# A decoder block with product-key experts: twelve more U chunks ahead, sixteen more gathered rows in the gate stage, and the gathered block closed inside the dense loop

## The chip, the cores and the metric

The kernel runs on one core of a Trainium2 chip. The metric is the device time of one execution, in microseconds (us); runs of the same kernel are compared by their median. The engines are named as in the profile: PE (TensorE, matmuls; PEld its weight loads), DVE (VectorE), ACT (ScalarE), POOL (GpSimd), and SP, whose queue issues most transfers.

## What is computed

The reference is one layer of a decoder block on x (1, 512, 1024) in float32. Its second half holds most of the work around the change:

```python
def peer_ffn(h, wq, subkeys, u, v):
    q = (h @ wq).reshape(B, S, PEER_HEADS, 2, PEER_QDIM // 2)
    sub_scores = jnp.einsum('bshpk,hpnk->bshpn', q, subkeys).astype(jnp.float32)
    ...
    best_v, best_pos = lax.top_k(cand, PEER_TOPK)
    expert = jnp.take_along_axis(cand_i, best_pos, axis=-1)
    gates = jax.nn.softmax(best_v, axis=-1).astype(h.dtype)
    ...
        ub = jnp.take(u, eb, axis=0)
        hid = jax.nn.gelu(jnp.einsum('tkd,td->tk', ub, xb), approximate=False) * gb
        vb = jnp.take(v, eb, axis=0)
        return jnp.einsum('tk,tkd->td', hid, vb)
...
    h2 = rms_norm(x, norm2_w[l]) * (1.0 + scale2) + shift2
    x = x + gate2 * peer_ffn(h2, peer_wq[l], peer_subkeys[l], peer_u[l], peer_v[l])
return rms_norm(x, final_norm_w)
```

Each token picks 8 x 16 = 128 of 16384 experts; an expert is a row of U and a row of V. Ahead of it stand windowed attention, gated linear attention and their projections, which the change does not touch.

## The kernel before

The 512 tokens are four blocks of 128. Three of them (DENSE, blocks 0 to 2) are computed densely: all experts for all tokens, with a gate of zero where an expert wasn't chosen. The fourth (GB, block 3) is gathered: for each of the 128 choices s an indirect transfer on POOL's queue fetches one row of U per token (gu, L993), DVE forms the dot product with the token (L1003), ACT the gelu of eight such columns at a time (hg, L1006), a second transfer fetches the rows of V (gv, L1011), and DVE adds them, weighted, to gacc (L1016). The last 16 tokens of block 2 have their U side done by gathered rows too (the sp rows, L964).

The 16384 experts are 128 chunks of 128. For a chunk c, u_part (from L691) loads U, splits it into a high and a low half (hilo: ACT writes uc..h at L64, DVE the difference uc..l at L65), runs 24 matmuls of 128x368 into ph (L69 to L71), and takes ACT's gelu (ge, L705). v_part (from L1149) splits V the same way (vc..h, vc..l), multiplies the gates with ge (DVE L1169), and splits the product into Ah (ACT L1173) and Al (DVE L1174). v_matmuls runs 18 matmuls of 128x512 into six accumulators acc0 to acc5, two for each dense block. High and low halves share a ring of four tiles between U and V chunks; Ah and Al have four buffers each.

The work runs in stages. A front (about 290 us) with the attention; the routing heads and top-k; a gate stage (about 460 to 705 us) that builds the dense gates: gate_group (from L904) makes one-hots on DVE (o12 at L895, o2 at L911), multiplies them on PE (pg, L918), copies them on ACT (gs, L920) and stores them in DRAM (Gd). Then the dense stage (from about 736 us) goes over the chunks in order.

U chunks can be done ahead of the dense stage, since U needs no gates. AHEAD lists them: all 64 even chunks. Their gelu results go to DRAM (gsp) and come back as gel tiles. The first 11 are done beside the routing heads; the others are woven into the gate stage by a balance: every piece of work has a DVE and a PE price, and a U chunk is put in where PE's sum lags behind DVE's, by the totals DVE_ALL and PE_ALL. The first 8 gathered rows of U are fetched and multiplied in the third block of the gate stage, one for each q (a q is a group of 16 tokens). The odd U chunks are done in the dense loop, LEAD = 8 chunks ahead of their V chunk, one for every two V chunks. The remaining gathers are dealt out evenly over the chunks (gather_to), up to chunk 123.

After chunk 123 finish(GB) forms the gathered block's result: times the second gate, plus x (L1192, L1193), ACT's squares (L1194), their root by ACT's logarithm and exponential and five small DVE steps (rstd_of, L80 to L86), the scaling (L1203; for one block L1200 on ACT and L1201 on POOL), and the store. The last four chunks (LAST) run block by block, each followed by its finish.

On DVE and POOL the order in the gate stage is that of the code (manual_schedule); elsewhere a scheduler with a simulated timeline orders each engine's instructions at build time, and each engine then runs its list in that order. A wait that an instruction needs holds all that stands behind it on its engine.

Of the kernel before, what the change touches and what calls it, by code (L numbers as in the profile page):

```python
# [7 lines left out]
F32 = mybir.dt.float32  # L8
# [9 lines left out]
P = 128  # L18
# [11 lines left out]
GB = 3  # L30
TG = 16
NGRP = TD // TG
TS = 16
TU = TD - TS
NGU = TU // TG
# [3 lines left out]

AHEAD = tuple(range(0, P, 2))  # L40
RING = 6
# [5 lines left out]
def peer_block_kernel(ctx: ExitStack, tc: tile.TileContext, a: dict, out: bass.AP):  # L47
    nc = tc.nc
    cp = ctx.enter_context(tc.tile_pool(name="cp", bufs=1, side="left"))
    st = ctx.enter_context(tc.tile_pool(name="st", bufs=1, side="left"))  # L50
    dr = ctx.enter_context(tc.tile_pool(name="dr", bufs=1, space=bass.MemoryType.DRAM))
# [636 lines left out]

    gsp = dr.tile([len(AHEAD), P, TU], F32, name="gsp")
    ges, last_gelu = {}, {}  # L690

    def u_part(c, lo_eng=None, after=None):
# [12 lines left out]
        last_gelu["u"] = nc.scalar.activation(gef, ph, AF.Gelu)  # L705
        if c % 2 == 0:
            nc.scalar.dma_start(gsp[c // 2], gef)
        else:
            ges[c] = ge
# [267 lines left out]
    NS = P  # L977
# [10 lines left out]

    EARLY = 8

# [27 lines left out]

    VLAG = 10
    gathers = [(s * 0.88 / NS, gather_u, s) for s in range(NS)]  # L1020
    gathers += [((s + VLAG) / (NS + VLAG), gather_v, s) for s in range(NS)]
    gathers = [g[1:] for g in sorted(gathers, key=lambda g: g[0])]

    def gather_to(upto):
        while gather_to.n < min(upto, len(gathers)):
            f, s = gathers[gather_to.n]
            f(s)
            gather_to.n += 1
# [54 lines left out]
    def ahead(s0, n):  # L1083
        for s in range(s0, s0 + n):
            fetch_u(s)
        yield 0, 0

    def dots_of(s0, n):
        gather_to(s0 + n)
        yield 1.15 * n, 0  # L1090

    def woven(n, rows, extra):
        for q in range(P // TG):
# [4 lines left out]
            if q in extra:  # L1098
# [6 lines left out]
                    6: [gate_parts(SB)], 7: [gate_rest(SB)]}  # L1105
    third_block = {0: [ahead(0, 1)]}
    for q in range(1, EARLY):
        third_block[q] = [dots_of(q - 1, 1), ahead(q, 1)]
    third_block[EARLY - 1] += [dots_of(EARLY - 1, 1)]
    work = chain(route_heads(), *head, woven(0, rows, first_block), woven(1, rows, second_block),  # L1110
                 woven(SB, [], third_block))
    NL_U = len(AHEAD) - LAST_U
    DVE_ALL = 11 + 4 * 7.6 + 3 + 1.15 * TS + 2.82 * 2 * NGRP + 9 + 1.14 * (NL_U - WQ_U)
    PE_ALL = 1.4 * 2 * NGRP + 3 + UCOST * (NL_U - WQ_U)
# [34 lines left out]
    def v_part(c):  # L1149
# [10 lines left out]
        vh, vl = hilo(v_part.raw[:, c % 2], [P, D], f"vc{c}", nc.vector)  # L1160
        if c % 2 == 0:
            if c % 4 == 0:
                v_part.ge = dnA.tile([P, 2, TU], F32, tag="gel", bufs=2, name=f"gel{c}")
                nc.sync.dma_start(v_part.ge, gsp[c // 2:c // 2 + 2].rearrange("c p t -> p c t"))
            ge = v_part.ge[:, c // 2 % 2].rearrange("p (g t) -> p g t", g=NGU)
        else:
            ge = ges.pop(c)
# [6 lines left out]
        nc.vector.tensor_tensor(grp(Al), A, grp(Ah), OP.subtract)  # L1174
        return c, Ah, Al, vh, vl

    def v_matmuls(parts, blocks=range(len(DENSE)), qs=(0, 1)):
# [27 lines left out]

    LEAD = 8
    for c in range(1, 1 + LEAD, 2):
        u_part(c)
    for c in range(P - LAST):
        if c % 2 == 0 and c + 1 + LEAD < P:  # L1210
            u_part(c + 1 + LEAD)
        with tc.issue_after(last_gelu["u"].ins) if c < 2 else nullcontext():
            parts = v_part(c)
        v_matmuls([parts])
        gather_to(len(gathers) * (c + 1) // (P - LAST))
        if c == 16:
            tc.keep_in_program_order(bcast_load(fwb, a["fw"], D))
        if c == P - 16:
# [4 lines left out]
            for q in range(2):  # L1223
# [3 lines left out]
                nc.scalar.activation(h2n[:, q * 512:(q + 1) * 512], pb, AF.Copy)  # L1227
    with tc.issue_after(last_gelu["u"].ins), tc.issue_after(last_gelu["hg"].ins):
        nc.scalar.preload_act_table_set("natural_log_exp_and_others")
    finish(GB, [gacc[:, 0:512], gacc[:, 512:1024]])  # L1230
    last = [v_part(c) for c in range(P - LAST, P)]
# [64 lines left out]
```

## Time and profile before

| | |
|---|---|
| median of 3 runs | 1524.5 us (1523.61 to 1525.55) |
| the profiled execution | 1523.26 us |
| its span, first to last instruction | 1521.5 us, mean granted clock 0.991 |
| PE busy | 1460.3 us (96%) |
| DVE busy | 1251.6 us (82%) |
| ACT busy | 677.7 us (45%) |
| POOL busy | 482.2 us (32%) |
| bytes moved | 417.04 MB, mean 274 GB/s |

All times in the views are of the profiled execution, from its span's start. A row of the timeline has the start, the duration, the engine, the line, the operation with output and inputs, and in brackets the idle time ahead of it with what ended it. A row of the groups has the busy time, the mean of one, and the idle time ahead. A row of the waits has who waited for whom, the total, the number and the longest. Matmul ends are modelled, and some matmul records are missing from the trace.

### The profile page before, as it was taken

The page shows a single profiled execution, that of the slowest core. Times are in us where ns is not written, and L with a number is a line of the kernel's source. Part 1 is how long each engine was busy: PE and PEld are TensorE (multiplying, and loading weights), DVE is VectorE, ACT ScalarE, POOL GpSimd, SP SyncE. Part 2 cuts the span into 40 slices and gives each one's busy share as a digit, 9 for nine tenths or more (in the row PEclk, how much of TensorE's full clock was granted, in tenths as well). Part 3 has the DMA queues.
Part 4 walks back from the last instruction along what each step waited for, and adds up shares of the span by engine and source line. Part 5 has one row for each costly group of instructions (what it writes and reads, how often), then busy time and mean ns, then how long its engine had stood idle before and what let it go on. Part 6 is the DMA issues. An engine that isn't in the chain of part 4 may idle for free.

```text
span 1521.5 us, 24401 instructions
## 1 busy us (share of the span) xinstructions
PE 1460.3 (96%) x9387; PEld 1301.7 (86%) x9387; DVE 1251.6 (82%) x2389; ACT 677.7 (45%) x1072; POOL 482.2 (32%) x344
## 2 busy tenths in 40 slices
PE   4999989899999999999999999999999999999995
PEld 3787877888999999999888888888888888888884
DVE  7578657689999999996778878787878878788998
ACT  5545486533344665765333333333333333333332
POOL 1000000145505220222334434453535434454461
PEclk9999999999999999999999999999999999999997
DMA  9253535462446997899999989989999898998894
GB/s 349 99 208 115 175 106 191 152 215 92 140 171 207 305 314 229 257 295 330 411 408 335 334 317 345 357 322 333 343 349 344 326 339 344 357 335 291 312 356 157
DMA packets 158004, 417.04 MB, mean 274 GB/s; under 512 B 11312, under 2 KB 78144, under 8 KB 145472
## 3 DMA queue, kind: packets, MB, share of 16 engines
q1 hardware_dynamic: 107296, 258.18, 47.5%
q0 software_dynamic: 39312, 144.20, 25.9%
q10 hardware_dynamic: 11280, 13.11, 2.5%
q8 instruction: 73, 1.20, 0.3%
q14 instruction: 43, 0.35, 0.1%
HBM read 374.01 MB, written 41.42 MB: 273 GB/s over the span
## 4 chain that ended last, share of the span: by engine, by line
PE 89%; DVE 4%; ACT 3%; DMA 2%; issue 2%; SPq 0%; DVEq 0%; POOL 0%; ACTq 0%; POOLq 0%
PE ph L71 11%; PE ph L69 11%; PE acc L70 11%; PE acc L69 11%; PE ph L70 11%; PE acc L71 11%; PE pg L918 4%; PE pq L69 2%; PE pq L71 2%; PE pq L70 2%; PE pj L71 1%; PE pj L69 1%; PE pj L70 1%; DMA gu<-in_u_dram,ix_u 1%; PE pn L69 1%
## 5 line engine op out<-in xcount | busy, mean ns | idle before, releaser
L993 POOL DMA_INDIRECT gu<-in_u_dram,ix_u x128 | 191.4, 1495 | 314.4 <-DVE gacc L1016 128.8
L1011 POOL DMA_INDIRECT gv<-in_vP_dram,ix_v x128 | 176.8, 1381 | 216.2 <-DVE gu L1003 163.9
L1173 ACT ACTIVATE Ah<-gr 128x384 fp32r<-128x384 f32 x128 | 67.1, 525 | 308.6 <-PE acc L70 305.0
L1016 DVE SCALAR_TENSOR_TENSOR gacc<-gv,hg,gacc 128x1024 f32<-128x1024 f32 x127 | 162.8, 1282 | 0.2
L1003 DVE SCALAR_TENSOR_TENSOR gu<-gu,h2n 128x1024 f32<-128x1024 f32 x128 | 156.0, 1220 | 0.7 <-DMA gu<-in_u_dram,ix_u 0.7
L705 ACT ACTIVATE ge<-ph 128x368 f32<-128x368 f32 x128 | 59.9, 468 | 152.8 <-PE ph L71 152.7
L1174 DVE TENSOR_TENSOR Al<-gr,Ah 128x384 fp32r<-128x384 f32 x128 | 71.0, 556 | 66.4 <-ACT Ah L1173 66.2
L920 ACT ACTIVATE gs<-pg 128x512 f32<-128x512 f32 x96 | 94.1, 1114 | 3.8 <-PE pg L918 2.8
L1066 POOL IOTA iot<- 128x256 bf16 x1 | 1.5, 1540 | 282.2 <-DVE h2Tl L680 282.2
L911 DVE TENSOR_TENSOR o<-o,gp 128x3072 bf16<-128x3072 bf16 x48 | 84.0, 1755 | 0.4 <-PE pg L918 0.4
L959 POOL DMA_INDIRECT spr<-in_u_dram,spix x16 | 40.6, 2535 | 105.6 <-DVE spr L964 61.3
L918 PE MATMUL pg<-o,o 128*128 128x128 bf16 x1152 | 72.7, 218 | 0.5 <-ACT gs L920 0.5
L918 PEld LDWEIGHTS <-o 128*128 128x128 bf16 x1152 | 66.2, 97 | 6.0 <-issue 0.7
L895 DVE TENSOR_TENSOR o<-iot,t 128x2048 bf16<-128x2048 bf16 x48 | 58.4, 1223 | 2.4 <-PE pg L918 2.4
L1169 DVE TENSOR_TENSOR gr<-ge,gr 128x368 f32<-128x368 f32 x64 | 34.5, 540 | 23.3 <-ACT ge L705 23.3
L217 DVE SCALAR_TENSOR_TENSOR macc<-wa,scs,macc 128x1024 f32<-128x1024 f32 x28 | 38.8, 1385 | 5.1 <-DMA wa<-in_w_ada_dram 4.8
L1169 DVE TENSOR_TENSOR gr<-gel,gr 128x368 f32<-128x368 f32 x64 | 31.9, 535 | 2.9 <-DMA gr<-Gd 2.9
L70 PE MATMUL pq<-h2Tl,wq_0h 128*128 128x512 f32 (+1 forms) x80 | 27.9, 349 | 1.2 <-DVE h2Tl L680 1.2
L69 PE MATMUL pq<-h2Th,wq_0h 128*128 128x512 f32 (+1 forms) x80 | 28.0, 352 | 1.0 <-ACT qha L758 1.0
L71 PE MATMUL pq<-h2Th,wq_1l 128*128 128x512 f32 (+1 forms) x80 | 28.1, 352 | 0.0
L70 PE MATMUL pq<-h2Tl,wq_1h 128*128 128x512 f32 (+1 forms) x80 | 28.1, 352 | 0.0
L69 PE MATMUL pq<-h2Th,wq_1h 128*128 128x512 f32 (+1 forms) x80 | 28.0, 350 | 0.0
(2608 smaller groups left out, 5028.3 us busy)
## 6 DMA issues: line engine op xcount, KB each, us to landing
u<-in_uT_dram SPq DMA_DIRECT2D x64, 1024.0 KB, 8.3
v<-in_vP_dram SPq DMA_DIRECT2D x64, 1024.0 KB, 7.5
Gd<-gs SPq DMA_DIRECT2D x23, 1024.0 KB, 8.1
gr<-Gd SPq DMA_DIRECT2D x15, 1536.0 KB, 11.0
wa<-in_w_ada_dram SPq DMA_DIRECT2D x20, 1024.0 KB, 6.3
gsp<-ge ACTq DMA_DIRECT2D x64, 184.0 KB, 4.6
gel<-gsp SPq DMA_DIRECT2D x32, 368.0 KB, 4.8
wi<-in_w_in_dram SPq DMA_DIRECT2D x9, 1024.0 KB, 6.2
```

What stands on the lines that cost most here:

```text
L69: nc.tensor.matmul(acc, lh, rh, start=start, stop=False)
L70: nc.tensor.matmul(acc, lh, rl, start=False, stop=False)
L71: return nc.tensor.matmul(acc, ll, rh, start=False, stop=stop)
L911: nc.vector.tensor_tensor(o2, o12[:, :, 1, None].to_broadcast([P, H, 3, P, 2]), gp3[:, g0:g0 + H, :, None].to_broadcast([P, H, 3, P, 2]), ...
L918: nc.tensor.matmul(pt[:, i, :], o12[:, g, 0, :, r], o2[:, g, m, :, r], start=(m == 0), stop=(m == 2))
L920: nc.scalar.activation(gs[:, :, t0 + 4 * f:t0 + 4 * f + 4].rearrange("p b a -> p a b"), pt, AF.Copy)
L993: nc.gpsimd.indirect_dma_start(out=ur, out_offset=None, in_=a["u"], in_offset=bass.IndirectOffsetOnAxis(ap=ix_u[:, s:s + 1], axis=0))
L1003: nc.vector.scalar_tensor_tensor(ur, ur, 1.0, h2n, op0=OP.mult, op1=OP.mult, accum_out=hid[:, s:s + 1])
L1011: nc.gpsimd.indirect_dma_start(out=vr, out_offset=None, in_=a["vP"], in_offset=bass.IndirectOffsetOnAxis(ap=ix_v[:, s:s + 1], axis=0))
L1016: nc.vector.scalar_tensor_tensor(gacc, vr, hg[:, s:s + 1], gacc, op0=OP.mult, op1=OP.add)
L1173: nc.scalar.activation(grp(Ah), A, AF.Copy)
L1174: nc.vector.tensor_tensor(grp(Al), A, grp(Ah), OP.subtract)
```

## The change

Six groups of four chunks (m = 3, 8, 13, 18, 23, 28) have their two odd U chunks done ahead as well: 13, 15, 33, 35, 53, 55, 73, 75, 93, 95, 113, 115. gsp and the gel tiles are arranged for it. The gathered rows of U in the gate stage go from 8 to 24, two for each of twelve places from the second block's q = 3 on. In the dense loop the gathers are dealt out by PE's time (4.09 for a V chunk, UCOST = 4.0 more where a U chunk goes along) and end with chunk 118; finish(GB) and the load of ACT's table for logarithm and exponential go into the loop at chunk 119.

```diff
-AHEAD = tuple(range(0, P, 2))
+ODD_AHEAD = tuple(range(3, 32, 5))
+AHEAD = tuple(c for m in range(P // 4) for c in (4 * m, 4 * m + 2) + ((4 * m + 1, 4 * m + 3) if m in ODD_AHEAD else ()))
...
-    gsp = dr.tile([len(AHEAD), P, TU], F32, name="gsp")
+    gsp = dr.tile([P // 4, 2, 2, P, TU], F32, name="gsp")
...
-        if c % 2 == 0:
-            nc.scalar.dma_start(gsp[c // 2], gef)
+        if c in AHEAD:
+            nc.scalar.dma_start(gsp[c // 4, c % 2, c // 2 % 2], gef)
...
-    EARLY = 8
+    EARLY = 24
...
-    VLAG = 10
-    gathers = [(s * 0.88 / NS, gather_u, s) for s in range(NS)]
-    gathers += [((s + VLAG) / (NS + VLAG), gather_v, s) for s in range(NS)]
+    gathers = [(-1, gather_u, s) for s in range(EARLY)]
+    gathers += [((s - EARLY) * 0.88 / (NS - EARLY), gather_u, s) for s in range(EARLY, NS)]
+    gathers += [((s + 0.5) / NS, gather_v, s) for s in range(NS)]
...
-    third_block = {0: [ahead(0, 1)]}
-    for q in range(1, EARLY):
-        third_block[q] = [dots_of(q - 1, 1), ahead(q, 1)]
-    third_block[EARLY - 1] += [dots_of(EARLY - 1, 1)]
+    third_block = {}
+    places = [(second_block, q) for q in range(3, 8)] + [(third_block, q) for q in range(P // TG)]
+    for i, (block, q) in enumerate(places):
+        pieces = block.setdefault(q, [])
+        if i:
+            pieces.append(dots_of(2 * i - 2, 2))
+        if i < EARLY // 2:
+            pieces.append(ahead(2 * i, 2))
+    assert EARLY == 2 * len(places) - 2
...
-    DVE_ALL = 11 + 4 * 7.6 + 3 + 1.15 * TS + 2.82 * 2 * NGRP + 9 + 1.14 * (NL_U - WQ_U)
+    DVE_ALL = 11 + 4 * 7.6 + 3 + 1.15 * TS + 2.82 * 2 * NGRP + 1.15 * EARLY + 1.14 * (NL_U - WQ_U)
...
-            if c % 4 == 0:
-                v_part.ge = dnA.tile([P, 2, TU], F32, tag="gel", bufs=2, name=f"gel{c}")
-                nc.sync.dma_start(v_part.ge, gsp[c // 2:c // 2 + 2].rearrange("c p t -> p c t"))
-            ge = v_part.ge[:, c // 2 % 2].rearrange("p (g t) -> p g t", g=NGU)
+        if c in AHEAD:
+            if c % 4 < 2:
+                v_part.ge[c % 2] = dn.tile([P, 2, TU], F32, tag=f"gel{c % 2}", bufs=2 - c % 2, name=f"gel{c}")
+                nc.sync.dma_start(v_part.ge[c % 2], gsp[c // 4, c % 2].rearrange("c p t -> p c t"))
+            ge = v_part.ge[c % 2][:, c // 2 % 2].rearrange("p (g t) -> p g t", g=NGU)
...
-    LEAD = 8
+    LEAD, LAST_G = 8, 118
+    cost = [4.09 + (UCOST if c % 2 == 0 and c + 1 + LEAD < P and c + 1 + LEAD not in AHEAD else 0) for c in range(LAST_G)]
     for c in range(1, 1 + LEAD, 2):
         u_part(c)
     for c in range(P - LAST):
-        if c % 2 == 0 and c + 1 + LEAD < P:
+        if c % 2 == 0 and c + 1 + LEAD < P and c + 1 + LEAD not in AHEAD:
             u_part(c + 1 + LEAD)
         with tc.issue_after(last_gelu["u"].ins) if c < 2 else nullcontext():
             parts = v_part(c)
         v_matmuls([parts])
-        gather_to(len(gathers) * (c + 1) // (P - LAST))
+        gather_to(EARLY + int((len(gathers) - EARLY) * sum(cost[:c + 1]) / sum(cost) + 1e-6))
+        if c == LAST_G + 1:
+            with tc.issue_after(last_gelu["u"].ins), tc.issue_after(last_gelu["hg"].ins):
+                nc.scalar.preload_act_table_set("natural_log_exp_and_others")
+            finish(GB, [gacc[:, 0:512], gacc[:, 512:1024]])
...
-    with tc.issue_after(last_gelu["u"].ins), tc.issue_after(last_gelu["hg"].ins):
-        nc.scalar.preload_act_table_set("natural_log_exp_and_others")
-    finish(GB, [gacc[:, 0:512], gacc[:, 512:1024]])
```

Where the order moves. The line numbers of the changed kernel are higher by 1 (hilo, u_part) to 8 (finish). On ACT around V chunk 28, before (vc28h is the high half of V chunk 28, Ah that of the gates, ge37 the gelu of U chunk 37):

```order
L705 ACTIVATE ge33_9548<-ph33_9523 128x368
L64 ACTIVATE vc26h_9657<-v26_9653 128x1024
L1173 ACTIVATE Ah28_9765<-gr3_9247 128x384
L64 ACTIVATE vc27h_9690<-v26_9653 128x1024
L1173 ACTIVATE Ah29_9798<-gr3_9247 128x384
L64 ACTIVATE uc37h_9725<-u37_9723 128x1024
L705 ACTIVATE ge35_9651<-ph35_9626 128x368
L1173 ACTIVATE Ah30_9864<-gr3_9247 128x384
L64 ACTIVATE vc28h_9758<-v28_9756 128x1024
L64 ACTIVATE vc29h_9793<-v28_9756 128x1024
L1173 ACTIVATE Ah31_9900<-gr3_9247 128x384
```

And of the change:

```order
L65 ACTIVATE uc37h_10059<-u37_10057 128x1024
L1179 ACTIVATE Ah29_10135<-gr3_9651 128x384
L1179 ACTIVATE Ah30_10198<-gr3_9651 128x384
L1179 ACTIVATE Ah31_10234<-gr3_9651 128x384
L706 ACTIVATE ge37_10088<-ph37_10063 128x368
L1007 ACTIVATE hg_2440<-hid_2439 128x8
L65 ACTIVATE vc28h_10092<-v28_10090 128x1024
L65 ACTIVATE vc29h_10130<-v28_10090 128x1024
L65 ACTIVATE uc39h_10160<-u37_10057 128x1024
```

vc28h stood ahead of ge37 and Ah31, and now stands behind both and behind hg. On PE the last matmuls of U chunk 37 (into ph37) stand right ahead of V chunk 28, before:

```order
L69 MATMUL ph37_9729<-h2Th_2428,uc37h_9725 128x368
L70 MATMUL ph37_9729<-h2Tl_2429,uc37h_9725 128x368
L71 MATMUL ph37_9729<-h2Th_2428,uc37l_9726 128x368
L69 MATMUL acc0_8177<-vc28h_9758,Ah28_9765 128x512
L70 MATMUL acc0_8177<-vc28l_9759,Ah28_9765 128x512
L71 MATMUL acc0_8177<-vc28h_9758,Al28_9766 128x512
```

And of the change:

```order
L70 MATMUL ph37_10063<-h2Th_2428,uc37h_10059 128x368
L71 MATMUL ph37_10063<-h2Tl_2429,uc37h_10059 128x368
L72 MATMUL ph37_10063<-h2Th_2428,uc37l_10060 128x368
L70 MATMUL acc0_8625<-vc28h_10092,Ah28_10099 128x512
L70 MATMUL acc1_8626<-vc28h_10092,Ah28_10099 128x512
L70 MATMUL acc2_8627<-vc28h_10092,Ah28_10099 128x512
```

U chunk 37 is ahead of V chunk 28 in both; the changed kernel runs the six products with the high half first. Ahead of U chunk 37 it has V chunks 22 to 27 with no U chunk between 22 and 27; the same pattern stands at 42, 62, 82 and 102, and V chunks 3 to 6 follow each other too. On ACT around V chunk 6, before:

```order
L1173 ACTIVATE Ah6_8636<-gr0_8348 128x384
L64 ACTIVATE vc5h_8565<-v4_8528 128x1024
L1173 ACTIVATE Ah7_8669<-gr0_8348 128x384
L64 ACTIVATE uc15h_8598<-u13_8495 128x1024
L705 ACTIVATE ge13_8526<-ph13_8501 128x368
L1173 ACTIVATE Ah8_8739<-gr1_8439 128x384
L64 ACTIVATE vc6h_8631<-v6_8629 128x1024
L64 ACTIVATE vc7h_8664<-v6_8629 128x1024
```

And of the change:

```order
L706 ACTIVATE ge11_8895<-ph11_8870 128x368
L1179 ACTIVATE Ah6_9041<-gr0_8796 128x384
L1179 ACTIVATE Ah7_9071<-gr0_8796 128x384
L1179 ACTIVATE Ah8_9141<-gr1_8899 128x384
L1179 ACTIVATE Ah9_9176<-gr1_8899 128x384
L65 ACTIVATE vc6h_9036<-v6_9034 128x1024
L65 ACTIVATE vc7h_9066<-v6_9034 128x1024
```

vc6h now stands behind Ah9, which needs the buffer that V chunk 5 frees. At the end, on DVE around the gathered block's finish (y3 is its result, y0 to y2 those of the dense blocks), before:

```order
L1016 SCALAR_TENSOR_TENSOR gacc_8184<-gv125_14579,hg_2440,gacc_8184 128x1024
L1016 SCALAR_TENSOR_TENSOR gacc_8184<-gv126_14582,hg_2440,gacc_8184 128x1024
L1016 SCALAR_TENSOR_TENSOR gacc_8184<-gv127_14585,hg_2440,gacc_8184 128x1024
L1192 TENSOR_TENSOR y3_14589<-gacc_8184,h2n_2430 128x512 x2
L1192 TENSOR_TENSOR y0_14681<-acc0_8177,h2n_2430 128x512
L1192 TENSOR_TENSOR y0_14681<-acc1_8178,h2n_2430 128x512
L1192 TENSOR_TENSOR y1_14730<-acc2_8179,h2n_2430 128x512
L1192 TENSOR_TENSOR y1_14730<-acc3_8180,h2n_2430 128x512
L1193 TENSOR_TENSOR y3_14589<-y3_14589,xf3_14590 128x512 x2
```

And of the change:

```order
L1017 SCALAR_TENSOR_TENSOR gacc_8632<-gv127_14408,hg_2440,gacc_8632 128x1024
L1200 TENSOR_TENSOR y3_14499<-gacc_8632,h2n_2430 128x512 x2
L1180 TENSOR_TENSOR Al125_14657<-gr15_14237,Ah125_14656 128x384
L1201 TENSOR_TENSOR y3_14499<-y3_14499,xf3_14500 128x512
L66 TENSOR_TENSOR vc124l_14641<-v124_14638,vc124h_14640 128x1024
L1201 TENSOR_TENSOR y3_14499<-y3_14499,xf3_14500 128x512
L66 TENSOR_TENSOR vc125l_14652<-v124_14638,vc125h_14651 128x1024
L1180 TENSOR_TENSOR Al126_14668<-gr15_14237,Ah126_14667 128x384
L66 TENSOR_TENSOR vc126l_14663<-v126_14660,vc126h_14662 128x1024
L1203 TENSOR_TENSOR ssf3_14502<-ssf3_14502 128x1
```

The gathered rows (gacc) now end ahead of the low half of chunk 124, and y3's steps stand among the last chunks instead of behind them.

More of the change, by code (lines that the diff above doesn't have):

```diff
@@ L1160, in v_part @@
         vh, vl = hilo(v_part.raw[:, c % 2], [P, D], f"vc{c}", nc.vector)
-        if c % 2 == 0:
-            if c % 4 == 0:
-                v_part.ge = dnA.tile([P, 2, TU], F32, tag="gel", bufs=2, name=f"gel{c}")
-                nc.sync.dma_start(v_part.ge, gsp[c // 2:c // 2 + 2].rearrange("c p t -> p c t"))
-            ge = v_part.ge[:, c // 2 % 2].rearrange("p (g t) -> p g t", g=NGU)
+        if c in AHEAD:
[3 more added lines that the diff above has]
+            ge = v_part.ge[c % 2][:, c // 2 % 2].rearrange("p (g t) -> p g t", g=NGU)
         else:
@@ L1175, in v_part @@
         return c, Ah, Al, vh, vl
+    v_part.ge = {}
     def v_matmuls(parts, blocks=range(len(DENSE)), qs=(0, 1)):
```

## Prediction

> **What bounds the kernel now.** First the page's busy times, its chain of waits and the span:
>
> ```profile
> PE 1460.3 (96%) x9387; PEld 1301.7 (86%) x9387; DVE 1251.6 (82%) x2389; ACT 677.7 (45%) x1072; POOL 482.2 (32%) x344
> ...
> PE 89%; DVE 4%; ACT 3%; DMA 2%; issue 2%; SPq 0%; DVEq 0%; POOL 0%; ACTq 0%; POOLq 0%
> ...
> core 0: 1521.5 us, clock 0.991
> ```
>
> TensorE is 89% of the chain. Then the windows by stage (columns: us; busy and count of PE, PEld, DVE, ACT, POOL; granted clock; DMA share; GB/s) say whether it waits anywhere:
>
> ```profile
> 560.00:700.00 140.00, 139.22 (x1298) 135.61 (x1297) 131.17 (x122) 91.36 (x114) 23.56 (x10) 1.00 0.87 275
> ...
> 740.00:1440.00 700.00, 700.00 (x3432) 615.81 (x3431) 574.59 (x753) 254.10 (x360) 307.56 (x218) 1.00 0.92 342
> ```
>
> In the gate stage (upper row) PE is busy 139.22 of 140 us with DVE at 131.17; in the dense stage it is busy all of 700 us. So moving matmuls from the lower row to the upper one saves nothing by itself: PE is full in both. What can be saved is PE's idle time and what follows its last matmul. The list of PE's waits from 460 us to its end:
>
> ```profile
> PE acc L69 <- ACT Ah L1173: 1.9, 1, 1.9
> PE acc L69 <- ACT vc118h L64: 1.3, 1, 1.3
> PE ph L71 <- DVE uc124l L65: 1.0, 1, 1.0
> PE pg L918 <- ACT gs L920: 0.5, 1, 0.5
> PE tr L865 <- ACT gs L920: 0.3, 1, 0.3
> ```
>
> That is 5.0 us in all. And the end, by windows and by single instructions:
>
> ```profile
> 1503.06:1516.17 13.11, 0.00 (x0) 0.00 (x0) 12.28 (x36) 5.65 (x21) 2.93 (x2) 0.58 0.28 104
> 1516.17:1521.50 5.33, 0.00 (x0) 0.00 (x0) 0.00 (x0) 0.00 (x0) 0.00 (x0) 0.50 0.37 139
> ```
>
> ```profile
> 1502.44 0.39 PE L70 MATMUL acc<-vc127l,Ah 128*128 128x512 f32 x1
> 1502.67 0.39 PE L71 MATMUL acc<-vc127h,Al 128*128 128x512 f32 x1
> ```
>
> ```profile
> 1495.49 1.28 DVE L1016 SCALAR_TENSOR_TENSOR gacc<-gv,hg,gacc 128x1024 f32<-128x1024 f32 x1
> 1496.81 1.29 DVE L1192 TENSOR_TENSOR y<-gacc,h2n 128x512 f32<-128x512 f32 x2
> ...
> 1510.06 1.41 DVE L1203 SCALAR_TENSOR_TENSOR y<-y,rf0y,fwb 128x512 f32<-128x512 f32 x2
> ...
> 1512.74 3.43 DVE L1203 SCALAR_TENSOR_TENSOR y<-y,rf2y,fwb 128x512 f32<-128x512 f32 x2
> ```
>
> PE ends at 1502.67 + 0.39 = 1503.06; the span ends 18.44 us later, of which DVE is busy 12.28 of the first 13.11. DVE is the bound of the tail: the last gathered row is added at 1495.49, so the gathered block and the three dense blocks all finish after it.
>
> **The tail (gain).** More prices: two pieces of the chain of waits, then a short step of ACT and its scale of y1:
>
> ```profile
> 1505.65 1.33 ACT xl L1194 x4
> ...
> 1511.97 0.17 DVE rf2t L83
> ```
>
> ```profile
> 1511.50 0.20 ACT L81 ACTIVATE rf2y<-rf2m 128x1 f32<-128x1 f32 x1 [1.75 <-DVE y L1203]
> ...
> 1511.88 1.33 ACT L1200 ACTIVATE y<-y,rf1y 128x512 f32<-128x512 f32 x2
> ```
>
> In the new order the gathered block's steps stand ahead of the last chunk's low half, so they are done before PE ends. From PE's end on there is left, in the order of the new lists: the product with acc5 (half of the 1.29 of such a pair, 0.65), the scale of y0 (1.41), the last sum with x (the same shape, 0.65); then ACT's square (0.7 with its accumulator: 1.33 for two of each, above), ACT's scale of y1, which now stands ahead of the last logarithm and exponential (1.33), those two (0.2 each), six one-column steps (0.77 for four, from 1511.97 to 1512.74, and 0.3 for the others: 1.1), the scale of y2 (1.4 alone, 3.43 beside GpSimd as here).
>
> The sum is 0.65 + 1.41 + 0.65 + 0.7 + 1.33 + 0.4 + 1.1 + 1.4 = 7.6, or 9.7 with 3.43; 5.33 follows as now. That makes 13.0 to 15.0 for 18.44; I take 13.6, nearer to the lower end since GpSimd's share of y1 begins before the scale of y2 does and covers only part of it. **Gain 4.8 (3.4 to 5.4).**
>
> **The twelve U chunks (the new waits).** ACT runs its list in order. By the order of the changed kernel, between 22 and 28, 42 and 48 and so on, six V chunks follow each other with no U chunk; behind them the next chunk's high half stands behind an ACT step that needs PE to be done with all that comes before that chunk. Two places of the profile have that structure already. The first, at chunk 0, where the gelu of U chunk 9 stands ahead of vc0h (columns: start, us, engine and line, in brackets the idle time ahead and its releaser):
>
> ```profile
> 734.16 0.33 PE L71 MATMUL ph<-h2Th,uc9l 128*128 128x368 f32 x1
> 734.53 0.48 ACT L705 ACTIVATE ge<-ph 128x368 f32<-128x368 f32 x1 [3.52 <-PE ph L71]
> 734.90 1.05 ACT L64 ACTIVATE vc0h<-v 128x1024 fp32r<-128x1024 f32 x1
> ...
> 735.85 0.51 ACT L1173 ACTIVATE Ah<-gr 128x384 fp32r<-128x384 f32 x1
> 735.98 1.23 DVE L65 TENSOR_TENSOR vc0l<-v,vc0h 128x1024 fp32r<-128x1024 f32 x1 [0.40 <-ACT vc0h L64]
> ...
> 736.41 2.41 PE L69 MATMUL acc<-vc0h,Ah 128*128 128x512 f32 x6 [1.92 <-ACT Ah L1173]
> ```
>
> U's last matmul ends at 734.49; gelu and high half are done at 734.90 + 1.05 = 735.95, and with Ah PE starts at 736.41. Where Ah is done earlier, PE would start some 0.46 sooner: 1.92 − 0.46 = **1.46**. The second, at chunk 118, has Ah121 (which waits for the buffer that chunk 117 frees) ahead of vc118h:
>
> ```profile
> 1448.20 0.39 PE L71 MATMUL acc<-vc117h,Al 128*128 128x512 f32 x1
> ...
> 1449.92 1.66 PE L69 MATMUL acc<-vc118h,Ah 128*128 128x512 f32 x6 [1.33 <-ACT vc118h L64]
> ```
>
> The price there is **1.33**. One more price is that of the small gelu of the gathered rows:
>
> ```profile
> L1006 ACT ACTIVATE hg<-hid 128x8 f32<-128x8 f32 x14 | 2.9, 204 | 5.5 <-DVE gu L1003 5.2
> ```
>
> Now the new places, from the order: chunks 28, 48, 68, 88 and 108, each right behind U chunk 37, 57, 77, 97, 117 on PE, with the gelu of that chunk ahead of their high half on ACT: 5 × 1.46 = 7.3, and at 28 also the small hg gelu (0.2).
>
> Chunk 6 has Ah9 ahead of vc6h and chunk 5 ahead of it on PE: 1.33. At 118 the hg gelu comes in between (0.2), and all 18 matmuls of it now run at once. The six products with the high half take 1.4 (6 × 0.23, the spacing of the two V matmuls that end PE's work, above); the low half is due then. DVE has Al121 (0.56), a gathered row (1.28) and vc118l (1.23) to do from about 0.6 behind chunk 117's end, when Ah121 is done, so it is through at about 3.7; PE wants it at 1.53 + 1.4 = 2.9: 0.8 more. Together 1.0 over now.
>
> Sum of the new waits: 7.3 + 0.2 + 1.3 + 1.0 = **9.8** (each between 0, if the step ahead is done sooner than I read it, and 1.92, the longest such wait seen: 0 to 14). At chunk 0 the order of these steps is as before, at chunk 119 the broadcast of the second gate stands in between on PE and covers the same wait, and uc124's 1.0 I leave as it is.
>
> **The clock.** Behind chunk 0's wait the granted clock fell, behind chunk 118's it did not:
>
> ```profile
> 736.40:740.50 4.10, 4.08 (x11) 0.58 1.02 418
> ...
> 1452.00:1456.00 4.00, 4.00 (x26) 1.00 0.84 278
> ```
>
> At 0.58 for 4.1 us that is 4.1 × 0.42 = 1.7 us of matmul time lost after 1.92 idle, none after 1.33. The new waits lie near 1.46, nearer to the row without a loss, so I put no clock in the sum; at most it is 7 × 1.7 = 12. The Trainium skill ("TensorE: Matmul & The Clock Gate", Part 1: The HAM clock gate) has the half clock come after an idle window of about 3.4 us; by that rule none of these waits costs any clock and the sum stays as it is, but the trace has a loss after 1.92, so I do not lean on it.
>
> **The gate stage.** It takes over 12 U chunks, 24 matmuls each at 0.166 (734.16 less 734.00 in the row below), 48 us of PE, and 16 more gathered rows:
>
> ```profile
> 734.00 0.33 PE L70 MATMUL ph<-h2Tl,uc9h 128*128 128x368 f32 x1
> ...
> L1003 DVE SCALAR_TENSOR_TENSOR gu<-gu,h2n 128x1024 f32<-128x1024 f32 x128 | 156.0, 1220 | 0.7 <-DMA gu<-in_u_dram,ix_u 0.7
> ```
>
> DVE gets 16 × 1.22 + 12 × 1.22 (low halves, like vc0l's 1.23) = 34 us against PE's 48. In the upper window it was 131 against 139, so it stays under PE, and the stage grows by the 48 us that the dense stage loses: zero. The cover is that the rows land in time: two per q come into buffers that the one-hots share, and DVE, which issues its list in order, would stand at a dot with the next one-hot behind it, and PE behind that. So far it stood 0.7 us. Bounds: 0 to 0.7 × 3 = 2 at the seen rate, 5 if each of 12 places loses 0.4; I take 0. The transfers of the dense stage, by their issues:
>
> ```profile
> v<-in_vP_dram SPq DMA_DIRECT2D x64, 1024.0 KB, 7.5
> ...
> gr<-Gd SPq DMA_DIRECT2D x15, 1536.0 KB, 11.0
> ...
> gel<-gsp SPq DMA_DIRECT2D x32, 368.0 KB, 4.8
> ```
>
> Two V chunks take PE 36 × 0.227 = 8.2 us. In a stretch without U they bring 1 MB of V, 2.8 gathered rows of 0.5 MB (232 rows paced over 118 × 4.09 + 47 × 4.0 = 670 us), a quarter of a gr and up to one gel: 1.0 + 1.4 + 0.4 + 0.3 = 3.1 MB, 380 GB/s, against 342 on average in the lower window above and 418 at the fullest, below. Tight; V has two chunks' time of lead and lands in 7.5, so I take 0, at most 1 us per stretch, 6.
>
> **Sum.** 1523.26 (the profiled execution) + 9.8 − 4.8 = 1528.3; the median of the runs is 1.24 above that execution (1524.5), so 1529.5.
>
> **Rivals.** *Faster: ACT's waits are hidden.* ACT stands 288.6 us at Ah and 139.4 at the gelus for PE between 740 and 1440 without PE losing anything:
>
> ```profile
> ACT Ah L1173 <- PE acc L70: 288.6, 116, 3.6
> ...
> ACT ge L705 <- PE ph L71: 139.4, 52, 2.8
> ```
>
> If the new places are like these, with the high half of the next chunk done earlier, only the tail counts: 1524.5 − 4.8 = 1519.7, or 1520.7 with chunk 118's 1.0. It decides below a total of 4.8 − 3.05 = 1.75 us, 0.25 for each of seven places. Against it: at the two places of the same structure the wait was there in full. 0.17. *The same:* half of the waits hold, 4.9 − 4.8: 1524.6. 0.15. *Slower still:* some 1.5 us waits bring the half clock (three of them 5.1), or loads in the U-free stretches or the gathered rows in the gate stage come late (5): 1533 to 1540, say 1534.6. For it: DMA near its highest seen rate; against it: no such wait at 740 to 1440 so far. 0.18. *The change does not do what it says,* so that the gathered block still ends last: gain 0, 1534.3; the order has it ahead of the last chunk's low half, so this counts within the last case.
>
> **How the numbers follow.** My forecast (all waits, tail as priced) has 0.50, with a range of its own of 1526 to 1533. A measurement of this kernel tells about 0.2%, 3.05 us, from no change. Slower: 0.50 + 0.18 = 0.68; same 0.15; faster 0.17. The range from 1520.5 to 1536.5 leaves out half of the faster case and a third of the slowest.
>
> **What would show it.** PE's list of waits in the changed kernel should have seven lines of 1.3 to 2.4 us, at acc, for vc6h, vc28h, vc48h, vc68h, vc88h, vc108h and vc118h (or their low halves), beside chunk 0's 1.9 and uc124's; the windows should have granted clock 1.00 behind them; PE's last matmul should end near 1513, and the span 13 to 15 us behind it with no step of the gathered block in between. I am wrong on the waits if PE is idle under 2 us more than the 5.0 of now, wrong on the tail if it is still over 16, and wrong on the gate stage if PE waits there for dots or one-hots by more than 2 us, or if the clock falls behind more than one new wait.

## The result and the profile after

The changed kernel takes 1545.13 us (median of 4 runs, 1543.73 to 1546.55), against 1525.03 (1523.61 to 1527.14) for the kernel before: a ratio of 1.0132 with an interval of 1.0117 to 1.0146. The direction was forecast, the size was not: 20 us slower where 5 were forecast, and above the range's upper end of 1536.5. Its profiled execution takes 1543.73 us with a span of 1542.0.

First PE's waits in the changed kernel, from 300 us on:

```profile
PE acc L72 <- DVE Al L1180: 4.2, 1, 4.2
...
PE acc L70 <- ACT Ah L1179: 1.9, 1, 1.9
PE acc L70 <- ACT vc28h L65: 1.6, 1, 1.6
...
PE acc L70 <- ACT vc48h L65: 1.5, 1, 1.5
PE acc L70 <- ACT vc68h L65: 1.5, 1, 1.5
PE acc L70 <- ACT vc88h L65: 1.5, 1, 1.5
PE acc L70 <- ACT vc108h L65: 1.5, 1, 1.5
PE acc L70 <- ACT vc118h L65: 1.4, 1, 1.4
PE acc L70 <- ACT vc6h L65: 1.4, 1, 1.4
...
PE acc L71 <- DVE vc118l L66: 0.5, 1, 0.5
```

The seven forecast waits are all there, at the forecast chunks and within 0.2 us of their prices except at 118, where the low half came 0.5 late and not 0.8. Two things were not forecast in this list: the 4.2 us for Al at the top, and that uc124's 1.0 us is gone (the two small waits for gs, 0.5 and 0.3, are gone too).

The Al wait is at chunk 0. The timeline of DVE there, then the issue of that gel tile on SP's queue:

```profile
790.61 0.99 DVE L1175 TENSOR_TENSOR gr<-gel,gr 128x368 f32<-128x368 f32 x2 [4.74 <-DMA gel<-gsp]
791.51 0.55 DVE L1180 TENSOR_TENSOR Al<-gr,Ah 128x384 fp32r<-128x384 f32 x1
```

```profile
769.28 1.20 SPq L1170 DMA_DIRECT2D gel<-gsp  x2
```

DVE stands 4.74 us at the gate product of chunks 4 and 6, whose gel tile is issued at 769.3 and lands some 21 us later, among 3 MB of V and 3 MB of gates; Al0, which PE wants, is behind it. In the kernel before, the same two products stand ahead of Al0 as well, but nothing waits for them:

```profile
727.50 0.54 DVE L1169 TENSOR_TENSOR gr<-gel,gr 128x368 f32<-128x368 f32 x1
```

This is the second of the two (the first starts at 725.42), without idle time ahead, almost 10 us before Al0 at 737.13. There the first two gel tiles lie in a pool that is open early, and are issued at 319.2 and 403.7 us; the change moved them into the dense pool, where the first is issued at 767.35.

The end, by windows (columns as before):

```profile
1529.43:1537.85 8.42, 0.00 (x0) 0.00 (x0) 6.60 (x16) 2.24 (x6) 2.48 (x2) 0.77 0.34 125
1537.85:1542.00 4.15, 0.00 (x0) 0.00 (x0) 0.08 (x1) 0.00 (x0) 0.00 (x0) 0.50 0.34 126
```

PE's last matmul ends at 1529.43, and the span 8.42 + 4.15 = 12.57 us later: 5.87 less than the 18.44 of before (4.8 forecast).

So PE ends 1529.43 − 1503.06 = 26.4 us later and the tail gives 5.9 back: 20.5, the difference of the spans. The waits make 4.2 + 1.4 + 1.6 + 4 × 1.5 + (1.4 + 0.5 − 1.3) − 1.0 = 12.8 of the 26.4. Most of the rest is in no list of waits: PE works, only slower. Here the first and the last of the 18 matmuls of V chunk 105, before and after, from the timelines:

```profile
1377.37 0.39 PE L69 MATMUL acc<-vc105h,Ah 128*128 128x512 f32 x1
...
1381.22 0.39 PE L71 MATMUL acc<-vc105h,Al 128*128 128x512 f32 x1
```

```profile
1402.99 0.40 PE L70 MATMUL acc<-vc105h,Ah 128*128 128x512 f32 x1
...
1406.94 0.39 PE L72 MATMUL acc<-vc105h,Al 128*128 128x512 f32 x1
```

17 spacings take 3.85 us before and 3.95 after: 226.5 and 232.4 ns (226.7 and 232.9 from unrounded times). The median over all V matmuls is 227 and 232 ns, the mean 228.4 and 233.1; the U matmuls stay at 167. With 18 × 128 = 2304 V matmuls the means make 2304 × 4.7 ns = 10.8 us. 12.8 + 10.8 = 23.6, and 2.8 of the 26.4 are left open. They lie in the dense stage: chunk 0 starts 48.0 us later (784.42 for 736.41), which is the time of the twelve U chunks, so the 1.6 us by which the first U chunk starts later are made up before it. Over all traces here that first start lies between 294.2 and 302.4, so the front part alone spreads by 8 us between executions.

No weight or V half was made differently, and the tail's V matmuls, where little DMA is left, are as slow (23 spacings from 1523.69 to 1529.03, 232 ns). One more thing in which the two programs differ is where their tiles lie in SBUF, the memory that holds them. The change moved the gel tiles from one pool into the dense pool; in the built programs Ah and Al, the weights of the V matmuls (what PEld loads), begin at byte 224 modulo 512 of the partition before and at 352 after, while all V halves, the other or moving operand, lie at 480 in both.

### The profile page after: what moved, and what is told of

Its sections match the earlier page's. It is cut to its first block, busy times and chain, and to the rows that moved or that the text cites. A ratio compares the mean times of both kernels' runs of the same rounds, so it can differ in the third digit from the quotient of the medians.

```text
span 1542.0 us, 24384 instructions
## 1 busy us (share of the span) xinstructions
PE 1475.1 (96%) x9387; PEld 1304.0 (85%) x9387; DVE 1252.2 (81%) x2389; ACT 678.8 (44%) x1072; POOL 473.6 (31%) x344
## 4 chain that ended last, share of the span: by engine, by line
PE 86%; DVE 5%; DMA 3%; ACT 3%; issue 2%; SPq 0%; DVEq 0%; POOL 0%; ACTq 0%; POOLq 0%
PE acc L70 11%; PE acc L72 11%; PE acc L71 11%; PE ph L70 10%; PE ph L72 10%; PE ph L71 9%; PE pg L919 3%; PE pq L70 2%; PE pq L72 2%; PE pq L71 2%; DMA gel<-gsp 1%; PE pj L72 1%; PE pj L70 1%; PE pj L71 1%; PE pn L70 1%
## 5 line engine op out<-in xcount | busy, mean ns | idle before, releaser
L994 POOL DMA_INDIRECT gu<-in_u_dram,ix_u x128 | 186.6, 1458 | 321.5 <-DVE gacc L1017 126.7
L1012 POOL DMA_INDIRECT gv<-in_vP_dram,ix_v x128 | 172.5, 1347 | 212.8 <-DVE gu L1004 126.5
L1175 DVE TENSOR_TENSOR gr<-gel,gr 128x368 f32<-128x368 f32 x76 | 36.9, 535 | 17.4 <-DMA gr<-Gd 10.8
L1175 DVE TENSOR_TENSOR gr<-ge,gr 128x368 f32<-128x368 f32 x52 | 27.8, 538 | 12.2 <-ACT ge L706 12.2
L71 PE MATMUL pq<-h2Tl,wq_0h 128*128 128x512 f32 (+1 forms) x80 | 27.9, 349 | 1.2 <-DVE h2Tl L681 1.2
```

The source lines that it names most:

```text
L71: nc.tensor.matmul(acc, lh, rl, start=False, stop=False)
L994: nc.gpsimd.indirect_dma_start(out=ur, out_offset=None, in_=a["u"], in_offset=bass.IndirectOffsetOnAxis(ap=ix_u[:, s:s + 1], axis=0))
L1012: nc.gpsimd.indirect_dma_start(out=vr, out_offset=None, in_=a["vP"], in_offset=bass.IndirectOffsetOnAxis(ap=ix_v[:, s:s + 1], axis=0))
```

## The experiments

### The place of the weights

The theory: V matmuls slow down because of where Ah and Al lie. The rival: the new traffic or order slows them. One kernel undoes that and one does only that, with an unused tile at the end of the dense pool. The pad moves every tile of that pool, but of these the V matmuls read only Ah and Al; the order of instructions on every engine is kept.

```diff
-    xl = dn.tile([P, 2, D], F32, tag="vraw", bufs=2, name="xl")
+    xl = dn.tile([P, 2, D], F32, tag="vraw", bufs=2, name="xl"); dn.tile([P, 32], F32, name="pad")
```

> The changed kernel with an unused tile of 128 bytes per partition at the end of the dense pool, so that all tiles of that pool lie 128 bytes lower: Ah and Al start at 224 modulo 512 as in the kernel before, instead of 352. Every engine's order is the same. Theory (place of the weights in SBUF): V matmuls go back from 232 to 227 ns spacing, 2304 of them, so about 11.6 us less: 1533.5. Rival (the new traffic or the new order slows the V matmuls): spacing stays at 232 and the time at 1545.

The same line with 96 in place of 32, in the kernel before:

> The kernel before with an unused tile of 384 bytes per partition in the same place, so that Ah and Al start at 352 modulo 512 as in the changed kernel; nothing else. Theory (place): V matmuls go from 227 to 232 ns, 11.6 us more: 1536.6. Rival (traffic or order): 1525, spacing 227.

Measured: the changed kernel with the pad 1534.65 us (median of 6, 1527.09 to 1539.16), a ratio of 1.0056 (1.0037 to 1.0076) to the kernel before instead of 1.0132; the kernel before with the pad 1536.12 (median of 4), a ratio of 1.0069 (1.0049 to 1.0089), beside 1524.71 for the kernel before. Chunk 105 in the two, changed kernel first:

```profile
1400.23 0.39 PE L70 MATMUL acc<-vc105h,Ah 128*128 128x512 f32 x1
...
1404.09 0.39 PE L72 MATMUL acc<-vc105h,Al 128*128 128x512 f32 x1
```

```profile
1388.96 0.39 PE L69 MATMUL acc<-vc105h,Ah 128*128 128x512 f32 x1
...
1392.92 0.40 PE L71 MATMUL acc<-vc105h,Al 128*128 128x512 f32 x1
```

3.86 and 3.96 us: 227 and 233 ns. The pad alone takes the 10.5 us away from one kernel (1545.13 − 1534.65) and adds 11.4 to the other (1536.12 − 1524.71). The rival, by which neither pad would change anything, falls.

Which property of the place counts was asked of four more places, all in the kernel before with pads of 64, 128, 224 and 256 bytes, one execution each.

> The kernel before with Ah and Al 64 bytes lower, at 160 modulo 512. At 224 the V matmuls stood 227 ns apart, at 352 they stood 232. If what counts is the distance from the moving operand (480 modulo 512 for all V halves; 256 good, 128 bad), 160 is a distance of 320: no worse than 227 if only near addresses disturb. If what counts is the address modulo 256 (224 good, 96 bad), 160 lies between: 227 to 232.

> The kernel before with Ah and Al 128 bytes lower, at 96 modulo 512. By address modulo 256 (352 is 96 too): 232 ns, 11 us more. By distance from the moving operand modulo 512 (384, that is 128 the other way): 232 if near counts in both directions, 227 if not.

> The kernel before with Ah and Al 224 bytes lower, at 0 modulo 512, on a boundary of 512 bytes. If a start off a boundary costs (224 less than 352): below 227 ns, down to 218, 10 to 20 us less. If only the distance from the moving operand counts (32): 232 or more.

> The kernel before with Ah and Al 256 bytes lower, at 480 modulo 512, the same residue as the moving halves of V. By address modulo 256 (224): 227 ns, no change. By distance from the moving operand (0): 232 or more.

And of the other operand: 128 bytes ahead of the ring of halves in the kernel before, which moves the V halves (moving operand of V) and the U halves (weights of U) from 480 to 96 modulo 512; then the same with Ah and Al moved as well, from 224 to 96.

```diff
-    hl = ctx.enter_context(tc.tile_pool(name="hl", bufs=1, side="left", reuse_waits="tile"))
+    hl = ctx.enter_context(tc.tile_pool(name="hl", bufs=1, side="left", reuse_waits="tile")); hl.tile([P, 32], F32, name="pad")
```

> The kernel before with 128 bytes in front of the ring of high and low halves, so that those tiles lie at 96 modulo 512 instead of 480, and Ah and Al stay at 224. The ring's tiles are the moving operand of the V matmuls and the weights of the U matmuls. If the place of the weights counts: V stays at 227 ns, U goes from 167 to about 172 (15 us more). If the distance between weights and moving operand counts: V goes to 232 (distance 128), and U, whose moving operand stays at 288, changes by its own distance.

> The kernel before with the ring of halves at 96 modulo 512 as in the run on the ring, and Ah and Al at 96 as well, 128 bytes lower than before. If what counts for V is the distance between weights and moving operand, it is 0 modulo 256 again: 227 ns, and U, whose operands lie as in the run on the ring, stays at 169 to 171: about 1531. If each operand's own place counts: V stays at 236 or gets slower, 1545 or more.

| V's weights, moving operand (byte modulo 256) | apart | one time, us | its kernel before | V spacing, median and mean, ns |
|---|---|---|---|---|
| 224, 224 (the kernel before) | 0 | 1523.26 | | 227, 228.4 |
| 224 (480 modulo 512), 224 | 0 | 1523.49 | 1524.77 | 227, 228.1 |
| 96, 96 | 0 | 1530.39 | 1522.85 | 227, 228.3 |
| 160, 224 | 64 | 1527.55 | 1524.77 | 229, 229.4 |
| 96, 224 (the changed kernel's) | 128 | 1538.4 | 1524.77 | 232, 232.7 |
| 224, 96 | 128 | 1545.03 | 1525.2 | 236, 233.8 |
| 0, 224 | 224 | 1536.09 | 1524.77 | 232, 233.3 |

V's spacing follows the distance of the two operands modulo 256: at 0 it is 227 wherever the pair lies (224 or 96), at 64 it is 229, and at 128 or 224 (32 the other way) the median is 232 to 236 and the mean 232.7 to 233.8. The times are of single executions; the spacings come from some 2240 pairs of matmuls each. The first four places alone fit a rule for the weights' own address modulo 256 as well, since the moving operand did not move in them; the last two decide for the distance, 236 with the ring alone moved and 227 again with both moved. A boundary of 512 bytes for the weights (row of 0) is no help, and the distance modulo 512 does not decide, since 480 and 224 are as good as each other. Two chunks of the last two kernels, the ring alone moved and both moved:

```profile
1396.84 0.40 PE L69 MATMUL acc<-vc105h,Ah 128*128 128x512 f32 x1
...
1400.81 0.39 PE L71 MATMUL acc<-vc105h,Al 128*128 128x512 f32 x1
```

```profile
1384.13 0.39 PE L69 MATMUL acc<-vc105h,Ah 128*128 128x512 f32 x1
...
1387.99 0.39 PE L71 MATMUL acc<-vc105h,Al 128*128 128x512 f32 x1
```

3.97 and 3.86 us. In the two kernels with the moved ring the U matmuls, whose moving operand h2T stays at 32 modulo 256, have a mean of 170.3 and 170.4 ns instead of 168.2: 128 × 24 × 2.2 ns = 6.8 us, about the 7.5 us that the kernel with both at 96 is slower (1530.39 for 1522.85). For U the moving operand lies 64 ahead of the weights in the kernel before (32 for 224) and 64 behind them with the ring moved; for V 64 ahead (224 for 160) costs 1 to 2 ns. Whether U at 167 has nothing left to gain was not tried.

The Trainium skill ("SBUF — State Buffer", Who interferes with whom) gives TensorE two independent read ports, one for the moving operand and one for the weights, and says that it never waits on anyone. That is said of other engines, and no run here contradicts it; between the two operands of TensorE itself, 128 bytes more or less are worth about 5 ns of each V matmul. Whether that arises at these ports is not shown.

### The parts of the change

The tail's part alone, in the kernel before: gathers by PE's time and done by chunk 118, the gathered block closed at chunk 119.

```diff
-    LEAD = 8
+    LEAD, LAST_G = 8, 118
+    cost = [4.09 + (UCOST if c % 2 == 0 and c + 1 + LEAD < P else 0) for c in range(LAST_G)]
...
-        gather_to(len(gathers) * (c + 1) // (P - LAST))
+        gather_to(EARLY + int((len(gathers) - EARLY) * sum(cost[:c + 1]) / sum(cost) + 1e-6))
+        if c == LAST_G + 1:
...
+            finish(GB, [gacc[:, 0:512], gacc[:, 512:1024]])
```

> The kernel before with the tail's part alone: gathers dealt out by TensorE's time, done by chunk 118, the gathered block closed at chunk 119; 8 early rows, even chunks ahead, Ah and Al at 224 as before. Theory (tail and new waits are separate terms): the tail falls by 5 to 6 us, no wait at 28, 48 and so on, no change of spacing: 1519.5. Rival (the gathers can't be done by 118 without the change's other parts, so DVE holds PE up in the dense stage): 1525 or more, with PE idle in the dense stage.

Measured: 1529.27 us, a ratio of 1.0024 (1.001 to 1.0038). The rival was right. Two of PE's waits in it, and its window from PE's end to the span's:

```profile
PE acc L69 <- ACT vc119h L64: 1.3, 1, 1.3
PE acc L69 <- ACT vc120h L64: 1.1, 1, 1.1
```

```profile
1509.74:1527.00 17.26, 0.00 (x0) 0.00 (x0) 10.18 (x29) 5.35 (x18) 2.48 (x2) 0.60 0.26 95
```

The tail falls by 1.2 us only, to 17.26, and PE waits 3.5 us more in the last chunks. The code hands the gathers out earlier, but DVE gets to them only a little earlier: its last gacc starts 13.1 us ahead of PE's end (1496.6 for 1509.74), where it was 7.6 (1495.5 for 1503.06), and in the changed kernel 27.9 (1501.5 for 1529.43). The block's last steps still fall among those of the first dense block. So the early close gains its 5.9 us only together with the sixteen rows that the dense stage no longer has; these are enough for it, since in the next kernel, without the odd chunks, the tail is 10.46 us (PE's last matmul ends at 1529.79, the span at 1540.25).

The changed kernel without the twelve odd chunks ahead:

```diff
-ODD_AHEAD = tuple(range(3, 32, 5))
+ODD_AHEAD = ()
```

> The changed kernel without the twelve odd U chunks ahead, all else as changed (24 early rows, pacing, end at 118, gel tiles in the dense pool); Ah and Al then lie at 224. Theory (waits come from the stretches without U): no wait at 6, 28, 48, 68, 88, 108, spacing 227, but the wait of Al0 at chunk 0 (4.2 us, gel tiles that can only be loaded once the dense pool is open) stays: 1521 to 1525. Rival (24 early rows need the extra U chunks, or PE waits for one-hots in the gate stage): 1530 or more, with PE idle at pg.

Measured: 1538.41 us, a ratio of 1.0084 (1.0066 to 1.0103). The rival again, with PE waiting in the gate stage, though at other places than it said:

```profile
PE ph L70 <- ACT ge L706: 10.9, 4, 4.8
PE ph L72 <- DVE uc124l L66: 2.3, 1, 2.3
...
PE ph L72 <- DVE uc112l L66: 1.8, 1, 1.8
PE trg L869 <- DMA gsp<-ge: 1.7, 1, 1.7
```

```profile
500.00:560.00 60.00, 56.17 (x523) 53.20 (x522) 59.85 (x59) 36.97 (x47) 16.95 (x10) 0.97 0.91 293
```

From 500 to 560 DVE is busy 59.85 of 60 us: with 24 early rows and no U chunks to go with them, this part of the gate stage is DVE's. From 600 to 765 DVE is busy about 77% and PE waits too; what holds it there was not followed up. In all PE is idle 19.7 of the 305 us from 460 to 765, and the granted clock falls in these windows, to 0.90 from 650 to 700. There is no wait at 6, 28, 48, 68, 88, 108, so those do come from the stretches without U; and no Al0 wait either, against my expectation. The timeline shows why: gel4 is late here too (its products stand 1.07 us for it, at 769.28), but they stand behind Al1 (767.66), so Al0 does not wait for them. The 4.2 us take both, the late tile and the place of its products ahead of Al0. The parts depend on each other: the rows leave room on DVE in the dense stage, the U chunks carry the rows in the gate stage, and the stretches that the U chunks leave behind hold the new waits.

### Taking the new waits away

The changed kernel with the pad, and its order mended. Its main lines, without the helpers that keep the instructions which `issue_after` names:

```diff
+        late = c in (28, 48, 68, 88, 108)
+        if late:
+            parts = v_part(c)
+            u_part.behind = c
...
+        with tc.issue_after(hilo.hi[f"vc{u_part.behind}"]) if u_part.behind else nullcontext():
+            last_gelu["u"] = nc.scalar.activation(gef, ph, AF.Gelu)
...
+        with tc.issue_after(v_part.al[{4: 1, 6: 1, 13: 6, 15: 6}[c]]) if c in (4, 6, 13, 15) else nullcontext():
+            nc.vector.tensor_tensor(A[:, :NGU], ge, A[:, :NGU], OP.mult)
...
+        with tc.issue_after(hilo.hi[f"vc{c - 3}"]) if c >= 9 else nullcontext():
+            nc.scalar.activation(grp(Ah), A, AF.Copy)
```

> The changed kernel with Ah and Al at 224 modulo 512 and with its new waits taken away by order alone: at chunks 28, 48, 68, 88, 108 V's split stands ahead of the U chunk and that chunk's gelu behind V's high half; every Ah stands behind the high half three chunks before its own; the gate products of chunks 4, 6, 13, 15 stand behind Al1 or Al6. Theory (waits 6 x 1.4, Al0 3.4 to 4.2, place 11 us make up the loss, and the tail's gain is real): PE idle falls from 16.4 to 5 us or less, and the time from 1534.7 to about 1522, 1 to 4 us under the kernel before. Rival (the waits come back elsewhere, DVE or DMA bounds the stretches without U): 1528 to 1535, with PE idle on DVE's low halves or on loads in these stretches.

Measured: 1525.87 us, a ratio of 1.0009 (0.9995 to 1.0024). 8.8 us less than with the pad alone, but 4 short of the expectation (about 1522); the rival's range (1528 to 1535) lies above. What is left of PE's waits, and ACT's wait at chunk 6:

```profile
PE acc L72 <- ACT vc6h L65: 4.6, 1, 4.6
PE acc L72 <- ACT vc28h L65: 2.8, 1, 2.8
...
PE acc L73 <- DVE vc108l L66: 1.4, 1, 1.4
PE acc L73 <- DVE vc48l L66: 1.2, 1, 1.2
```

```profile
814.69 1.06 ACT L65 ACTIVATE vc6h<-v 128x1024 fp32r<-128x1024 f32 x1 [7.20 <-DMA v<-in_vP_dram]
```

The waits for Al0, at 68 and at 118 are gone, and 88 is down to 0.4 and 0.4. At chunk 6 ACT now stands 7.2 us for V's load; at 28 vc28h stands behind the small hg gelu, which waits 5.33 us for DVE's dot products; at 48 and 108 DVE brings the low half late. So behind the order there were real limits at some of the places: the loads in the first stretch, DVE in the others; and the two long waits took the clock with them (last section). In sum PE's listed waits hardly fall: 13.1 us here, 15.7 with the pad alone. From chunk 0 to PE's end the mended kernel takes 732.7 us (781.63 to 1514.34) and the one with the pad alone 736.9 (787.93 to 1524.87), and the tail is 10.26 against 12.52; that makes 6.5 of the 8.8, and for the rest these two executions tell little, since their fronts alone differ by 6.7 us.

The last kernel takes these two up: ten odd chunks (13 and 15 back in the dense loop), and gathers dealt out by what is left of DVE and not by PE's time.

```diff
-ODD_AHEAD = tuple(range(3, 32, 5))
+ODD_AHEAD = tuple(range(8, 32, 5))
...
-    cost = [4.09 + (UCOST if ...
+    cost = [1.9 + (2.8 if ...
```

> The kernel with the mended waits (all as there), but ten odd U chunks ahead instead of twelve (13 and 15 stay in the dense loop, so no stretch without U at the start, where V's loads came late), and the gathers dealt out by what DVE has left instead of by TensorE's time (1.9 for a V chunk, 2.8 more with a U chunk), since DVE was late at chunks 28, 48 and 108. Theory (what was left there, 13.2 us of PE idle, was loads at chunk 6 and DVE in the stretches): no wait at chunk 6, at most 1 us each at 28, 48, 88, 108; 1516 to 1521, under the kernel before. Rival (the first stretch was not special, DMA is late in each): the wait moves to chunk 28 and the time stays at 1524 to 1528.

Measured: 1520.92 us, a ratio of 0.9971 (0.9959 to 0.9982): faster than both kernels, by 0.3% and 1.6%; the first is small, but its interval lies clear of 1. The profiled execution is the slowest of its twelve (1528.52 us; its first U chunk starts at 302.4, where it was 295.3 before), so only its waits are compared. Without chunk 0's 1.9 for Ah the longest are:

```profile
PE acc L72 <- ACT vc28h L65: 1.6, 1, 1.6
PE acc L73 <- DVE vc108l L66: 1.4, 1, 1.4
PE acc L73 <- DVE vc0l L66: 1.3, 1, 1.3
PE acc L73 <- DVE vc48l L66: 1.2, 1, 1.2
```

Chunk 6 has none, against the rival; at 28, 48 and 108 they are still over 1 us each, so there the expectation was too good, and chunk 0 has one more. What the ten chunks and what the new pacing did was not separated.

## Why the prediction was wrong

The direction came out as forecast, but not for the forecast's reasons alone: its own terms make 9.6 of new waits less 5.9 of tail, 3.7 us. The other 16 us were in no term of the sum and in none of the rivals.

- **Moved matmuls cost nothing in either place:** right for the U matmuls that were moved. Chunk 0 starts 48.0 us later (784.42 for 736.41), the twelve chunks' time.
- **The six new waits and 118:** right in place, cause and price: 1.4 + 1.6 + 4 × 1.5 = 9.0 measured, 8.8 forecast (7.3 + 0.2 + 1.3); at 118 0.6 more than before, 1.0 forecast. That they came from the stretches without U is shown by the kernel without the odd chunks, which has none of the six; that ACT's order held PE is shown by the kernel with the mended order, in which ACT's high half no longer holds it at 48, 68, 108 and 118. Mending that order does not win the whole price back: at 48 and 108 DVE's low half takes the place of ACT's wait, and at 6 and 28 the high half comes still later than in the changed kernel.
- **The tail:** 5.9 gained, 4.8 forecast and 5.4 its upper bound. y2's scale takes 1.4 and not 3.4: it starts at 1536.52, when GpSimd's two steps for y1 (1533.60 to 1536.08) are done. Two one-column steps beside GpSimd take 0.39 and 1.19 in its place, where the others take some 0.15, so DVE's part comes to 8.42, nearer to 7.6 than to 9.7. The stretch from DVE's end to the span's end is 4.15 us, not 5.33.
- **The step that failed: the V matmuls have no term in the sum.** The prediction carries their 0.227 us over to the changed kernel ("Two V chunks take PE 36 × 0.227 = 8.2 us") and adds only waits and the tail to the time of before, as if their duration were given by their shape. The change moved tiles, and with them the weights' place: 227 became 232 ns, 10.5 to 11.4 us by the two crossed runs, of the 15.6 us by which the measured time lies above the forecast. No view of the profile of before shows it and no order does; the place of the tiles in the built program does, and I had not compared it. That gel moved from one pool to another was in the diff.
- **A second miss: "At chunk 0 the order of these steps is as before".** That holds for ACT. On DVE the products with gel4 stand ahead of Al0 in both kernels, but now their tile is loaded late, 4.2 us of wait; the loads at the start of the dense stage had no term.
- **Loads in the stretches without U, taken at 0 of up to 6:** in the changed kernel nothing shows, where Al0's wait and ACT's order make PE late at chunk 6 in any case; with the order mended, 4.6 us came out there.
- **The clock:** right for the new waits: behind those of 1.4 to 1.6 us the granted clock is 1.00. In the dense stage it falls once, at chunk 0, by about as much as before, though here behind the 4.2 us for Al0:

```profile
792.10:796.20 4.10, 4.08 (x12) 3.13 (x13) 2.24 (x4) 1.58 (x2) 0.00 (x0) 0.64 1.03 419
```

The row that the forecast leaned on, the loss behind chunk 0's 1.92 us, turned out to be no fixed price (last section).

With the place undone the changed kernel comes to 1534.65, inside the range: of its 5.1 us above my 1529.5, Al0 is 3.4 in the profiled execution.

## What to carry to other kernels

When a change moves a tile to another pool, compare where every operand of the bound engine lies before and after, since a stream of matmuls can slow down with no wait anywhere; a pad of 128 bytes, and the spacing in its trace, tell in one profiled execution. Where an engine runs a list in order, look in the new order for what stands directly ahead of the step that the bound engine needs next: most of these prices came out to 0.2 us. Such a wait can hide others: only with the order mended did the late loads and DVE's late low halves show.

## What the runs showed of the hardware

- In these kernels the 128x512 matmuls with float32 data stand 227 ns apart (median) when weights and moving operand lie at the same byte modulo 256, 229 ns when they lie 64 bytes off, and 232 to 236 ns when they lie 128 or 224 bytes off; over 2304 of them 128 bytes made 10.5 and 11.4 us. What in the chip does this was not found.
- PE idle for up to 1.6 us left the granted clock at 1.00 at every new wait. Behind the 1.92 us ahead of chunk 0, which are the same in all fourteen profiled executions, it fell within 1.4 us in seven (to 0.58 over 4.1 us in the kernel before) and did not in the other seven (1.00 over the same 4.1 us in the kernel before with the pad of 384 bytes). What decides between the two was not found. It fell behind the changed kernel's 4.2 us (0.64 over 4.1 us), and in the mended kernel behind the 4.6 us at chunk 6 (0.63 over 4 us) and the 2.8 us at chunk 28. The window behind chunk 28 there, with the granted clock third from the end:

```profile
943.00:947.00 4.00, 4.00 (x11) 3.26 (x11) 4.00 (x5) 2.91 (x4) 3.39 (x3) 0.50 0.91 328
```

  The Trainium skill ("TensorE: Matmul & The Clock Gate", Part 1: The HAM clock gate) puts the loss behind an idle window of about 3.4 us; here 2.8 us were followed by one, 1.92 us in half of the executions, and 1.6 us in none.
